# A 64-row matmul into a spare PSUM bank after the second unit of each MLP part

## The chip, the cores and the metric

The kernel runs on one core of one Trainium2 chip. The metric is device time in microseconds (us), the median of several executions; less is better. One further execution was taken with the hardware profiler, and every row below is from that one.

## The reference

Two layers of a decoder trunk over 256 tokens of width 2048, in fp32. Each layer normalises, projects, mixes (attention and RWKV-7 in layer 0, RG-LRU and HGRN2 in layer 1), projects back, and then runs an MLP with a squared ReLU. The change touches the two MLPs alone:

```python
D_MODEL, SEQ, D_FF = 2048, 256, 4 * 2048

def _sq_relu_mlp(h, w1, w2):
    z = jax.nn.relu(h @ w1)
    return (z * z) @ w2

for layer in range(2):
    ...                                   # mixers: x = x + y
    x = x + _sq_relu_mlp(_rms_norm(x, norm_mlp[layer]), w_ff1[layer], w_ff2[layer])
```

## The kernel before

Activations lie transposed: 16 blocks of 128 features, each with 256 tokens. To keep fp32 accuracy, weights and activations are split into a high part and a low part (fp32r). A moving block is `[128, 256 high | 256 low]`.

A **unit** (`unit`, L155) makes one block of 128 output features. It runs 16 **pairs** of matmuls (`mm3`, L147), one pair for each block of the contraction: L152 multiplies the high weights with all 512 moving columns ("the high matmul"), and L153 the low weights with the 256 high columns ("the low matmul"). Each of them loads its own 128x128 weights first. The 32 matmuls of a unit accumulate in one bank of the PSUM pool `pmm`, which has two buffers. Afterwards `evac` (L163) adds the two halves through ScalarE and VectorE.

The weights of a unit come in two halves of 512 KB by SyncE's DMA queue (`load`), and ScalarE (L130) and VectorE (L132) split them. These loads and splits have a high priority, so they run ahead of the matmuls that use them.

`mlp` (L928) has eight **parts** of 16 units each: `up(0) up(1) down(0) up(2) down(1) up(3) down(2) down(3)`. An `up` makes a quarter of the hidden layer, a `down` adds a quarter's contribution to the trunk `xs`. One MLP is 128 units, or 2048 pairs, and both MLPs together are 256 units. Each engine runs its own instructions in order; a tile scheduler sets that order from priorities and from the order of the code.

Other PSUM banks come from `bank` (L112), the pool `pg` with the tags `ga` and `gb`, two buffers each. The mixers use them heavily; in the MLPs nobody does, apart from one matmul of `rstd_of` (L206) while the first unit runs. `ident` is a 128x128 fp32 identity in the tile `con`.

Matmuls whose operands are plain fp32 (not fp32r) appear in the mixers. The ones that matter below: L425 contracts over 64 rows of the array with 128 columns of weights, L520 has 64 moving columns with the whole array, L522 uses 128 rows and 64 columns, L600 128 rows and 32 columns, L477 32 rows and 32 columns, and L206 and L838 use the whole array. In a row of the trace, `64*128` ahead of the shapes says rows and columns of the array.

Of the kernel before, what the change touches and what calls it, by code (L numbers as in the profile page):

```python
# [58 lines left out]
def kernel(  # L59
# [58 lines left out]
    def operand(pool, name):  # L118
        """16 blocks [128, 256 high | 256 low] of a moving operand."""
        return [t[:, k] for t in (half_of(pool, f"{name}_{h}") for h in range(2)) for k in range(8)]  # L120

# [1 line left out]
    def load(src, h, name, pool=None):  # L123
# [11 lines left out]
    def stream(src, name, pool=None):  # L135
        """A chunk of 16 blocks [K 128, 128 columns], in parts of 8 blocks: (high, low) each."""
        out = []
        for h in range(2):
            with tc.high_priority():
                out.append(split(load(src, h, name, pool if h else None), h, name))  # L140
        return out

    def behind():
        """Work of the mixers that yields to the projections that are ready."""
        return tc.high_priority(-120)
# [25 lines left out]
    def sigmoid(dst, src, bias=0.0):  # L171
        """exp(-ln(1 + exp(-x))) of x = src + bias, with x held above -80 where exp(-x) would overflow"""
        V.tensor_scalar(dst, src, bias, -80.0, op0=ALU.add, op1=ALU.max)
        A.activation(dst, dst, AF.Exp, scale=-1.0)
        A.activation(dst, dst, AF.Ln, bias=one_b[: dst.shape[0]])
        A.activation(dst, dst, AF.Exp, scale=-1.0)
# [7 lines left out]

# [1 line left out]
    def rsqrt_of(dst, src, scale, bias, name, pool):  # L186
        """exp(-ln(scale * src + bias) / 2)"""
        l = pool.tile([src.shape[0], src.shape[1]], F32, tag="rsl", name=f"l_{name}", bufs=2 if pool.name == "pn" else 1)
        A.activation(l, src, AF.Ln, bias=bias[: src.shape[0]], scale=scale)
        A.activation(dst, l, AF.Exp, scale=-0.5)  # L190
# [39 lines left out]

# [1 line left out]
    def layer0_mix():  # L232
# [77 lines left out]
    def rwkv_a(pa, gate, hx, scaled, rwp_d, pm_d, nb, first, load_cw):  # L310
# [26 lines left out]
        for j in range(8):  # L337
# [18 lines left out]
            sigmoid(aa, ps2[:, :T], bias=p_("a0", j))  # L356
            # features
            cs = tl("cs", bufs=2, name=f"cs_{j}")
# [19 lines left out]
            with behind():  # L378
# [32 lines left out]
                A.copy(rwp[:, 1796:2052], psg[:, :T])  # L411
                # token major copies
                ptv = bk_(f"ptv_{j}")
# [5 lines left out]
                A.copy(rwp[:, 512:1024], ptb)  # L419
                # products within the chunks  # L420
                for q in range(2):
# [14 lines left out]
    def rw_solve(pb, nb, z_d):  # L436
        """(1 - N)^-1 of the strictly upper triangular N [32, 32] of every partition, in place."""
        for s in range(1, 31):
            n = 31 - s
            tmp = pb.tile([P, 2, T], F32, tag="y", name=f"ztmp_{s}")  # L440
            tv = tmp.rearrange("p r t -> p (r t)")[:, : s * n].rearrange("p (r t) -> p r t", t=n)
            V.tensor_mul(
                tv, nb[:, 0:s, s : s + 1].to_broadcast([P, s, n]),
                nb[:, s : s + 1, s + 1 : 32].to_broadcast([P, s, n]))
            V.tensor_add(nb[:, 0:s, s + 1 : 32], nb[:, 0:s, s + 1 : 32], tv)
        G.memset(nb.rearrange("p r t -> p (r t)")[:, 0 : 1024 : 33], 1.0)
        G.dma_start(z_d, nb)

    def rwkv_b(pb, j, rwp_d, pm_d, z_d, yr):
        """The chunks of two pairs of heads in turn, from the products within the chunks."""  # L450

# [36 lines left out]
        s = None  # L488
# [205 lines left out]

# [1 line left out]
    def layer1_mix(hx, rstd, ym):  # L696
        scaled = scaled_by(rstd)
        with ExitStack() as st:
            hp = st.enter_context(tc.tile_pool(name="hp", bufs=1))
            hgmk = hp.tile([P, 7, P], F32, name="hgmk")  # L700
            nc.scalar.dma_start(hgmk, hgmask)
            lw = hp.tile([P, 2, 8, P], F32, name="lw")
            nc.scalar.dma_start(lw, lru_w)
            prm = hp.tile([P, 8, 8], F32, name="prm")
            # lower bounds of the forget gates: softmax over the two layers
            mxl, e0, e1 = prm[:, 0], prm[:, 1], prm[:, 2]
            V.tensor_max(mxl, p_("lb0"), p_("lb1"))
            V.tensor_sub(e0, p_("lb0"), mxl)
            V.tensor_sub(e1, p_("lb1"), mxl)
            A.activation(prm[:, 1:3], prm[:, 1:3], AF.Exp)  # L710
            V.tensor_add(mxl, e0, e1)
            V.reciprocal(mxl, mxl)
            V.tensor_mul(e0, e0, mxl)
            V.tensor_mul(e1, e1, mxl)
            V.tensor_add(e1, e0, e1)
            lower, oml = prm[:, 1], prm[:, 2]
            V.tensor_sub(lower, e1, e0)
            V.tensor_scalar(oml, lower, -1.0, 1.0, op0=ALU.mult, op1=ALU.add)
            # softplus(-lambda) = max(-lambda, 0) + log1p(exp(-|lambda|)),
            # log1p(e) = 2 atanh(e / (2 + e)) as its series in s = e / (2 + e) <= 1/3  # L720
            sp = prm[:, 3]
            ab = prm[:, 4]
            V.tensor_scalar(ab, p_("lam"), -1.0, None, op0=ALU.mult)
            V.tensor_tensor(sp, ab, p_("lam"), ALU.min)
            A.activation(sp, sp, AF.Exp)
            s2, pl = prm[:, 5], prm[:, 0]
            V.tensor_scalar_add(s2, sp, 2.0)
            V.reciprocal(s2, s2)
            V.tensor_mul(sp, sp, s2)
            V.tensor_mul(s2, sp, sp)  # L730
            V.tensor_scalar(pl, s2, 1.0 / 19, None, op0=ALU.mult)
            for n in range(17, 1, -2):
                V.scalar_tensor_tensor(pl, pl, 1.0 / n, s2, ALU.add, ALU.mult)
            V.scalar_tensor_tensor(sp, pl, 1.0, sp, ALU.add, ALU.mult)
            V.tensor_scalar_max(ab, ab, 0.0)
            V.scalar_tensor_tensor(sp, sp, 2.0, ab, ALU.mult, ALU.add)
            V.tensor_scalar(prm[:, 4], sp, -8.0, None, op0=ALU.mult)
            V.tensor_scalar(prm[:, 5], sp, 8.0, None, op0=ALU.mult)

            at = [hp.tile([P, 384], F32, name=f"at{i}") for i in range(2)]  # L740
            for a in at:
                G.memset(a, 0.0)
            for h in range(8):
                hgrn_head(hp, h, hx, scaled, ym, hgmk, prm, at)
            for q in range(2):
                lru_group(hp, q, hx, scaled, ym, lw, prm)

    def hgrn_head(hp, h, hx, scaled, ym, hgmk, prm, at):
# [29 lines left out]
        with behind():  # L778
# [6 lines left out]
            a = at[h % 2]  # L785
            # pairs within blocks of 64
            for b in range(4):
# [23 lines left out]
                for x, m in enumerate(todo):  # L811
# [3 lines left out]
                    V.copy_predicated(dst, hgmk.bitcast(U32)[:, lvl, None, :].to_broadcast([P, 2, P]), src)  # L815
            # blocks of 64 and of 128 against each other
            eu = tl("he", bufs=2, name=f"heu_{h}")
# [37 lines left out]
    def lru_group(hp, grp, hx, scaled, ym, lw, prm):  # L855
# [5 lines left out]
        for j in js:  # L861
# [15 lines left out]
            scaled(unit(w_in1[33 + 2 * j], hx, f"i1_{33 + 2 * j}"), gate[j], f"lgt{j}")  # L877
        # the activations by table set, in this order
        pin = tc.keep_in_program_order
# [9 lines left out]
        act_set(LN_EXP)  # L889
        # 1 - exp(2 log a) = 2 t / (1 + t), t = tanh(-log a)  # L890
        d = {}
# [16 lines left out]

# [1 line left out]
    def out_proj(xs, w_out, ym, order, acc, hx, gain, name):  # L910
# [17 lines left out]
    def mlp(layer, xs, hx, rstd, nxt, zp, zraw):  # L928
        z = {}

        def up(q):
            zq = z[q] = operand(big if q % 2 == 0 else zp, f"z_{layer}_{q}")
            for k in range(KT):
                n = f"f1_{layer}_{q}_{k}"
                s = evac(unit(w_ff1[layer, q * KT + k], hx, n, pool=zraw), n)
                V.tensor_mul(s, s, rstd)  # L936
                V.scalar_tensor_tensor(s, s, 0.0, s, ALU.max, ALU.mult)
                split_to(zq[k], s)

        def down(q):  # L940
            for c in range(KT):
                n = f"f2_{layer}_{q}_{c}"
                s = evac(unit(w_ff2[layer, q, c], z[q], n, pool=zraw), n)
                V.tensor_add(xs[:, c], xs[:, c], s)
                if q == 3:
# [10 lines left out]

# [1 line left out]
    ym = layer0_mix()  # L958
# [26 lines left out]

# [1 line left out]
def _chunks(w):  # L987
    """[K, N] -> [N / 128, 128, K / 128 * 128]: for each 128 columns the blocks of K, side by side."""
    k, n = w.shape
# [11 lines left out]
def _layout(i):  # L1001
# [53 lines left out]

    # constants of the shapes alone
    con = np.zeros((P, NCON), f32)
# [69 lines left out]
```

## Time and profile before

| what | value |
|---|---|
| median of the timed runs | 2411.09 us (3 runs, 2410.25 to 2414.4) |
| span of the profiled execution | 2435.2 us |
| TensorE (PE) busy in it | 2409.9 us, 99% |
| VectorE, ScalarE busy | 1697.5 us, 1244.4 us |
| first MLP, its matmuls | from about 580 us to about 1304 us |
| second MLP, its matmuls | from about 1720 us to the end |

The profiled execution has a span, from its first instruction to its last; no other time of it is given. A row's start counts from the beginning of the span. PE stands for TensorE's matmuls, and the weight loads have rows of their own. Matmuls overlap in the array, so a matmul's duration is longer than the distance from its start to the next one's. That distance is what a stream of matmuls costs.

### The profile page before, as it was taken

Reading aid. Unit: us, or ns where it says so; the run is one execution under the profiler, and the core shown is the slowest. Engines: PE = TensorE matmul, PEld = TensorE weight load, DVE = VectorE, ACT = ScalarE, POOL = GpSimd, SP = SyncE. Lnnn points to the kernel's source line nnn. Section 1 sums busy time; section 2 is a strip of 40 time slices with the busy share of each in tenths; the row PEclk is TensorE's granted clock in tenths of the full one; section 3 lists DMA queues with packets and bytes.
Section 4 is the critical chain, followed back from the end, with each engine's and each line's share of the span. In section 5 each row is a group of like instructions: output and inputs, shape, how many; then the busy total and the mean of one; then the engine's idle time right before and its main releaser. Section 6 shows DMA issues by size and latency. Waiting matters only on the chain.

```text
span 2435.2 us, 37943 instructions
## 1 busy us (share of the span) xinstructions
PE 2409.9 (99%) x14385; PEld 2087.2 (86%) x14385; DVE 1697.5 (70%) x3006; ACT 1244.4 (51%) x2152; POOL 44.2 (2%) x115
## 2 busy tenths in 40 slices
PE   7999999999999999999999999999999999999999
PEld 6888877789888888888888888889988888888888
DVE  7887745677676566566567888788777667667555
ACT  7554335655444444444456666586544444444443
POOL 0111010000000000000000000000000000000000
PEclk9999989999999999999999999999999999999999
DMA  7666643365555555555555444456556655655564
GB/s 261 211 215 217 221 141 114 115 216 182 185 188 185 187 187 185 189 184 187 185 188 174 156 156 149 152 167 216 183 190 190 191 190 190 190 190 190 190 196 134
DMA packets 125861, 446.75 MB, mean 183 GB/s; under 512 B 14192, under 2 KB 19952, under 8 KB 124016
## 3 DMA queue, kind: packets, MB, share of 16 engines
q1 hardware_dynamic: 115824, 414.04, 53.0%
q0 software_dynamic: 5456, 26.79, 3.0%
q10 hardware_dynamic: 4400, 3.50, 0.4%
q8 instruction: 114, 1.87, 0.3%
q14 instruction: 67, 0.55, 0.1%
HBM read 429.04 MB, written 15.22 MB: 182 GB/s over the span
## 4 chain that ended last, share of the span: by engine, by line
PE 93%; DVE 3%; DMA 2%; ACT 1%; issue 1%; POOL 0%; DVEq 0%; POOLq 0%; SPq 0%; ACTq 0%
PE mm_f L152 39%; PE mm_f L153 20%; PE mm_i L152 13%; PE mm_i L153 7%; PE mm_o L153 2%; PE mm_o L152 2%; PE mm_o L149 1%; PE mm_o L150 1%; PE hl L810 1%; DVE wl_i L132 1%; PE pair L425 1%; PE psx L495 0%; DMA rwp_d<-rwp 0%; PE psu L502 0%; PE psx L493 0%
## 5 line engine op out<-in xcount | busy, mean ns | idle before, releaser
L132 DVE TENSOR_TENSOR wl_f<-raw_f,wh_f 128x1024 fp32r<-128x1024 f32 x512 | 627.2, 1225 | 486.1 <-ACT wh_f L130 486.1
L130 ACT CAST wh_f<-raw_f 128x1024 fp32r<-128x1024 f32 x512 | 538.6, 1052 | 772.9 <-PE mm_f L152 566.4
L152 PE MATMUL mm_f<-hx_m,wh_f 128*128 128x512 f32 x2048 | 717.2, 395 | 0.0
L152 PE MATMUL mm_f<-z,wh_f 128*128 128x512 f32 x2048 | 717.1, 395 | 0.0
L152 PE MATMUL mm_i<-hx_a,wh_i 128*128 128x512 f32 x1536 | 571.3, 409 | 13.1 <-ACT wh_i L130 13.1
L153 PE MATMUL mm_f<-hx_m,wl_f 128*128 128x256 f32 x2048 | 574.7, 281 | 0.0
L153 PE MATMUL mm_f<-z,wl_f 128*128 128x256 f32 x2048 | 574.3, 280 | 0.0
L152 PEld LDWEIGHTS mm_f<-hx_m,wh_f 128*128 128x128 f32 x2048 | 383.9, 187 | 90.0
L152 PEld LDWEIGHTS mm_f<-z,wh_f 128*128 128x128 f32 x2048 | 383.9, 187 | 90.0
L153 PE MATMUL mm_i<-hx_a,wl_i 128*128 128x256 f32 x1536 | 451.6, 294 | 1.3 <-DVE wl_i L132 1.2
L153 PEld LDWEIGHTS mm_f<-hx_m,wl_f 128*128 128x128 f32 x2048 | 387.0, 189 | 0.1
L153 PEld LDWEIGHTS mm_f<-z,wl_f 128*128 128x128 f32 x2048 | 387.0, 189 | 0.0
L152 PEld LDWEIGHTS mm_i<-hx_a,wh_i 128*128 128x128 f32 x1536 | 292.8, 191 | 76.0 <-ACT wh_i L130 14.0
L153 PEld LDWEIGHTS mm_i<-hx_a,wl_i 128*128 128x128 f32 x1536 | 294.3, 192 | 11.0 <-DVE wl_i L132 4.4
L132 DVE TENSOR_TENSOR wl_i<-raw_i,wh_i 128x1024 fp32r<-128x1024 f32 x192 | 234.6, 1222 | 92.2 <-ACT wh_i L130 85.9
L130 ACT CAST wh_i<-raw_i 128x1024 fp32r<-128x1024 f32 x192 | 201.3, 1049 | 183.4 <-PE mm_i L152 169.2
L168 DVE TENSOR_TENSOR s_f<-mm_f,t_f 128x256 f32<-128x256 f32 x256 | 106.7, 417 | 3.0 <-ACT t_f L167 3.0
L132 DVE TENSOR_TENSOR wl_o<-raw_o,wh_o 128x1024 fp32r<-128x1024 f32 x64 | 78.2, 1223 | 29.3 <-ACT wh_o L130 29.0
L130 ACT CAST wh_o<-raw_o 128x1024 fp32r<-128x1024 f32 x64 | 67.1, 1049 | 60.7 <-issue 31.1
L167 ACT COPY t_f<-mm_f 128x256 f32<-128x256 f32 x256 | 93.2, 364 | 4.3 <-PE mm_f L153 4.3
L153 PE MATMUL mm_o<-ym,wl_o 128*128 128x256 f32 x256 | 72.7, 284 | 0.9 <-DVE wl_o L132 0.9
L936 DVE TENSOR_TENSOR s_f<-s_f,rstd_m 128x256 f32<-128x256 f32 x128 | 54.4, 425 | 4.4
(418 smaller groups left out, 2274.7 us busy)
## 6 DMA issues: line engine op xcount, KB each, us to landing
raw_f<-in_w_ff_dram SPq DMA_DIRECT2D x512, 512.0 KB, 4.3
raw_i<-in_w_in_dram SPq DMA_DIRECT2D x192, 512.0 KB, 3.9
raw_o<-in_w_out_dram SPq DMA_DIRECT2D x64, 512.0 KB, 3.9
rwp_d<-rwp POOLq DMA_DIRECT2D x8, 1026.0 KB, 7.1
rwp<-rwp_d POOLq DMA_DIRECT2D x4, 1540.0 KB, 10.6
cw<-in_cmp_w_dram SPq DMA_DIRECT2D x2, 2048.0 KB, 9.2
pm_d<-pm POOLq DMA_DIRECT2D x8, 512.0 KB, 6.3
pm<-pm_d POOLq DMA_DIRECT2D x4, 1024.0 KB, 6.4
```

The lines of the kernel that those rows point to most:

```text
L130: A.copy(wh, raw)
L132: V.tensor_sub(wl, raw, wh)
L149: M.matmul(ps[:, :T], wh, mv[:, :T], start=first, stop=False)
L150: M.matmul(ps[:, :T], wh, mv[:, T:], start=False, stop=False)
L152: M.matmul(ps, wh, mv, start=first, stop=False)
L153: M.matmul(ps[:, :T], wl, mv[:, :T], start=False, stop=last)
L167: A.copy(t, ps[:, T:])
L168: V.tensor_add(s, ps[:, :T], t)
L425: M.matmul(pp[:, c * P : (c + 1) * P], bk[hs, c], ar[hs, c], start=True, stop=True)
L810: M.matmul(pl[:, x * T + i * P : x * T + (i + 1) * P], qk[:, ii], qk[:, ii], start=True, stop=True)
L936: V.tensor_mul(s, s, rstd)
```

## The change

After the second unit of every part (index 1), one matmul takes 64 rows of the identity as weights and 64 rows by 64 columns of it as the moving operand. It writes 128x64 numbers into a buffer of `ga`, and nothing reads them. `keep_in_program_order` ties the new matmuls to their place among themselves. There are 8 in each MLP, 16 in all. The other lines of the diff only drop comments.

```diff
     def mlp(layer, xs, hx, rstd, nxt, zp, zraw):
         z = {}
 
+        def narrow(n):
+
+            ps = bank(f"nar_{n}")
+            tc.keep_in_program_order(M.matmul(ps[:, 0:64], ident[0:64], ident[0:64, 0:64], start=True, stop=True))
+
         def up(q):
...
                 s = evac(unit(w_ff1[layer, q * KT + k], hx, n, pool=zraw), n)
+                if k == 1:
+                    narrow(n)
                 V.tensor_mul(s, s, rstd)
...
                 s = evac(unit(w_ff2[layer, q, c], z[q], n, pool=zraw), n)
+                if c == 1:
+                    narrow(n)
                 V.tensor_add(xs[:, c], xs[:, c], s)
```

In TensorE's order the first part of the second MLP read as follows before, where the second unit (`mm_f_1_0_1`) ends and the third (`mm_f_1_0_2`) begins:

```order
L152 MATMUL mm_f_1_0_1_17778<-hx_m_1_16665,wh_f_1_0_1_1_17787 128x512
L153 MATMUL mm_f_1_0_1_17778<-hx_m_1_16665,wl_f_1_0_1_1_17789 128x256
L152 MATMUL mm_f_1_0_2_17831<-hx_m_0_16664,wh_f_1_0_2_0_17834 128x512
L153 MATMUL mm_f_1_0_2_17831<-hx_m_0_16664,wl_f_1_0_2_0_17836 128x256
L152 MATMUL mm_f_1_0_2_17831<-hx_m_0_16664,wh_f_1_0_2_0_17834 128x512
```

With the change the same place on TensorE reads:

```order
L152 MATMUL mm_f_1_0_1_17794<-hx_m_1_16681,wh_f_1_0_1_1_17803 128x512
L153 MATMUL mm_f_1_0_1_17794<-hx_m_1_16681,wl_f_1_0_1_1_17805 128x256
L934 MATMUL nar_f_1_0_1_17843<-con 128x64
L152 MATMUL mm_f_1_0_2_17849<-hx_m_0_16680,wh_f_1_0_2_0_17852 128x512
L153 MATMUL mm_f_1_0_2_17849<-hx_m_0_16680,wl_f_1_0_2_0_17854 128x256
```

The new matmul (L934) stands exactly between the last low matmul of the second unit and the first high matmul of the third, and it names no wait. It is the same at all 16 places. Apart from these 16 rows, no engine's order differs, and the DMA queues' does not either.

## Rows read from the trace of the kernel before

**Rows 1.** The page: the span, the busy engines, and the granted clock in 40 slices
```profile
span 2435.2 us, 37943 instructions
...
PE 2409.9 (99%) x14385; PEld 2087.2 (86%) x14385; DVE 1697.5 (70%) x3006; ACT 1244.4 (51%) x2152; POOL 44.2 (2%) x115
...
PEclk9999989999999999999999999999999999999999
```

**Rows 2.** TensorE in two stretches, one inside each MLP: busy (matmuls), clock, DMA
```profile
600.00:1290.00 690.00, 690.00 (x3907) 1.00 0.58 186
1730.00:2420.00 690.00, 690.00 (x3983) 1.00 0.60 189
```

**Rows 3.** Groups by line, 600 to 1290 us: busy, mean ns, idle before
```profile
L152 PE MATMUL mm_f<-z,wh_f 128*128 128x512 f32 x984 | 347.8, 399 | 0.0
```

**Rows 4.** The same group, 1730 to 2425 us
```profile
L152 PE MATMUL mm_f<-z,wh_f 128*128 128x512 f32 x1009 | 349.9, 391 | 0.0
```

**Rows 5.** Groups by line, whole span: L206, which runs twice at `ms_m`
```profile
L206 PE MATMUL ms_m<-acc_m,con 128*128 128x256 f32 x4 | 1.4, 431 | 0.0
```

**Rows 6.** Timeline of TensorE around four 64-row matmuls: start, us, what
```profile
175.43 0.28 PE L153 MATMUL mm_i<-hx_a,wl_i 128*128 128x256 f32 x1
175.64 1.16 PE L425 MATMUL pair<-rwp,bk 64*128 64x128 f32 x8
176.72 0.50 PE L152 MATMUL mm_i<-hx_a,wh_i 128*128 128x512 f32 x1
177.06 0.28 PE L153 MATMUL mm_i<-hx_a,wl_i 128*128 128x256 f32 x1
```

**Rows 7.** Timeline around one fp32 matmul of 64 moving columns
```profile
343.43 0.43 PE L520 MATMUL psy<-rwp,st 128*128 128x64 f32 x2
343.79 0.34 PE L522 MATMUL psy<-pm,rwp 128*64 128x64 f32 x4
```

**Rows 8.** Timeline around one whole-array fp32 matmul of 128 columns, L838
```profile
1360.03 0.28 PE L153 MATMUL mm_i<-hx_a,wl_i 128*128 128x256 f32 x1
1360.15 0.38 PE L838 MATMUL hh<-hqs,hks 128*128 128x128 f32 x2
...
1360.60 0.28 PE L153 MATMUL mm_i<-hx_a,wl_i 128*128 128x256 f32 x1
```

**Rows 9.** Timeline around one whole-array fp32 matmul of 256 columns, L206
```profile
1310.56 0.28 PE L153 MATMUL mm_i<-hx_a,wl_i 128*128 128x256 f32 x1
...
1311.34 0.28 PE L153 MATMUL mm_i<-hx_a,wl_i 128*128 128x256 f32 x1
```

**Rows 10.** Groups by line, 178 to 187 us, right behind rows 6
```profile
L152 PE MATMUL mm_i<-hx_a,wh_i 128*128 128x512 f32 x24 | 8.5, 399 | 0.0
```

**Rows 11.** Groups by line, 254 to 264 us, behind L600, which ends at 252.6
```profile
L152 PE MATMUL mm_i<-hx_a,wh_i 128*128 128x512 f32 x24 | 8.5, 398 | 0.0
```

**Rows 12.** Timeline behind 32 matmuls of L477
```profile
392.89 0.39 PE L152 MATMUL mm_i<-hx_a,wh_i 128*128 128x512 f32 x1
...
393.23 0.40 PE L152 MATMUL mm_i<-hx_a,wh_i 128*128 128x512 f32 x1
```

**Rows 13.** Timeline around another four 64-row matmuls of L425
```profile
128.70 0.39 PE L152 MATMUL mm_i<-hx_a,wh_i 128*128 128x512 f32 x1
129.02 1.16 PE L425 MATMUL pair<-rwp,bk 64*128 64x128 f32 x8
130.11 0.39 PE L153 MATMUL mm_i<-hx_a,wl_i 128*128 128x256 f32 x1
```

**Rows 14.** Groups by line, 132 to 142 us, behind rows 13
```profile
L152 PE MATMUL mm_i<-hx_a,wh_i 128*128 128x512 f32 x30 | 10.4, 391 | 0.0
```

**Rows 15.** Groups by line, 1712 to 1722 us, ahead of L206
```profile
L152 PE MATMUL mm_f<-hx_m,wh_f 128*128 128x512 f32 x8 | 2.9, 399 | 0.0
```

**Rows 16.** Timeline: L206 in the first unit of the second MLP
```profile
1722.72 0.70 PE L206 MATMUL ms_m<-acc_m,con 128*128 128x256 f32 x2
```

**Rows 17.** Groups by line, 1724 to 1734 us, behind that L206
```profile
L152 PE MATMUL mm_f<-hx_m,wh_f 128*128 128x512 f32 x30 | 10.4, 391 | 0.0
```

## The prediction

> **What bounds the kernel now.** I read the page first. TensorE is busy 99% of the span, VectorE 70%, ScalarE 51% [rows 1]. So the question in the MLPs is how closely matmul follows matmul. Next I asked for one stretch inside each MLP. In both the engine is never idle and the granted clock is 1.00, the higher of its two levels, 2.4 GHz [rows 2]. No wait appears ahead of the MLPs' matmuls, the idle time before them is 0.0 [rows 3, 4]. Whatever TensorE gets on top in these stages, the time pays in full.
>
> The same two rows show something less expected. In 690 us the first MLP issues 3907 matmuls and the second 3983 [rows 2], with the same instructions, shapes and clock. Per pair that is 690 / (3907 / 2) = 353.2 ns against 690 / (3983 / 2) = 346.5 ns, a difference of 6.7 ns. The modelled duration of the high matmul tells the two cadences apart at a glance: 399 ns in the first MLP, 391 ns in the second [rows 3, 4]. I call them slow and fast. Each lasts through a whole MLP, and since nothing waits there, nothing can end it. The cadence a stream falls into seems to be decided where the stream is broken. At the head of the second MLP the high matmuls still show 399 [rows 15], then comes a single fp32 matmul, L206 [rows 16], and from there on it is 391 [rows 17]. The change breaks the stream 16 times, so it has two prices: that of the break, and that of the cadence afterwards.
>
> **The price of one break.** One plain fp32 matmul of the program is two records: L206 runs once in each layer at this tile, and the group counts four [rows 5]. So each `narrow` adds two weight loads and two matmuls of 64 columns. No row shows a lone matmul of this shape, but all its pieces are there. I measure from the start of the last low matmul of the second unit to the start of the first low matmul of the third. Without a break this is one pair, 0.347 us.
>
> - Into the 64-row shape. Ahead of L425, which uses 64 rows and 128 columns of the array as `narrow` does, 0.21 us pass from the low matmul's start to the first L425 [rows 6]. Between matmuls of the usual shape it is 0.12 us (1360.03 to 1360.15) [rows 8].
> - The two matmuls and the way back. L520 has the same 64 moving columns and is followed by a change of shape. From its first record to the first of L522 0.36 us pass [rows 7].
> - The restart. The first high matmul after L425 starts at 176.72 and its low matmul at 177.06, 0.34 us later [rows 6]. This is one weight load more than in the stream, because nothing could be loaded ahead.
>
> The sum is 0.21 + 0.36 + 0.34 - 0.347 = 0.56 us for each, and 16 of them are **9.0 us**. Nothing hides it, TensorE has no idle time there. Behind the break only the weight stream stands, on engines with 30% to 49% to spare.
>
> The lower bound is a matmul that changes no shape: L838 stretches the distance from low to low to 0.57 us [rows 8], which is 0.22 more than a pair, or 3.6 us for 16. For the upper bound I take L206, four times as many columns, at 0.78 - 0.35 = 0.43 us [rows 9]. To that I add what the two shape changes cost above: 0.21 - 0.12 = 0.09 in front, and 0.1 for emptying plus 0.1 for a bare weight load behind. That gives 0.72, or 11.5 us. I take 9.0, because L425 has the very shape of `narrow` and shows the front and the restart directly.
>
> Why the front and the restart cost so much is what a page states: the Trainium skill, in "TensorEngine Tiling (Array Packing)", Key Properties, says that going over to another tiling mode empties TensorE first. The 0.21 us against 0.12 above agrees, but the page has no price. Without that rule the sum would be the 3.6 us of L838, with it the 9.0 us of the rows.
>
> **The cadence after the break.** What comes behind `narrow` is always a high matmul, L152. The trace has three places where L425 is followed by L152 and a long stream, at 175.6, 202.8 and 229.1 us, and all three go on slow: 399 ns [rows 10] stands for the three. After 32 matmuls of L600, another narrow shape, again followed by L152, it is 398 [rows 11]. The exception is a short stretch of five pairs after L477, where the high matmuls stand 0.34 us apart [rows 12]: fast. Where L425 is followed by the low matmul instead [rows 13], the stream goes on fast, 391 [rows 14], at all five such places. So I expect that an emptied array that restarts with L152 goes on slow.
>
> The first MLP is slow already and gains or loses nothing by that. The second is fast now, and its two units ahead of the first `narrow` stay so. The remaining 126 units are 2016 pairs, and 2016 x 6.7 ns = **13.5 us**.
>
> **The sum.** 9.0 + 13.5 = 22.5 us. The profiled execution would go from a span of 2435.2 to about 2457.7 us. That execution is known by its span alone, which lies 24.1 us above the median of the timed runs, so I carry the difference over: 2411.1 + 22.5 = **2433.6 us**. What a measurement of this kernel can tell from no change is about 0.2%, 4.8 us.
>
> **The rivals.**
>
> - *The break decides for fast.* L206 at the head of the second MLP turned slow into fast [rows 15 to 17], and the five places of L425 with a low matmul behind went fast too. Against it stand the three places with the very order of the change. If all 16 breaks led to fast, the first MLP would win 13.5 us, the second would lose nothing, and with 9.0 us for the breaks the time would be 2411.1 - 4.5 = 2406.6 us. This is the case on the faster side. A part is worth about 256 x 6.7 ns = 1.7 us. Eight parts are slow now, so with n slow parts the change is 9.0 + (n - 8) x 1.7, and it is a gain only when two or fewer of 16 stay slow. I give it 0.18.
> - *The cadence doesn't matter.* The timed runs may not have two cadences (they are 24.1 us shorter than the span), or the breaks may leave about as many parts slow as before. Then the breaks alone remain: 2411.1 + 9.0 = 2420.1 us. The three timed runs lie within 4.2 us, so no MLP went from one cadence to the other among them, which speaks for neither side. I give it 0.25. By a page's rule it would come out this way: the Trainium skill, "TensorE: Matmul & The Clock Gate", Back-to-back issue gap, gives for a warm array a distance that depends on the columns alone. The trace differs, 353.2 against 346.5 ns with the same columns and clock.
> - *The timed runs were fast in both MLPs, and the change makes both slow.* Then 9.0 + 2 x 13.5 = 36.0 us are lost, 2447 us. The shorter timed runs would fit, but nothing else shows it: 0.07.
> - *The break is cheap.* If the shape change costs nothing between matmuls that wait for nobody, 3.6 us and an untouched cadence give 2414.7 us, which is no measurable change. [rows 6] speak against it, although L425 there may have waited for its inputs. I give it 0.05. That the change does nothing at all is excluded, the 16 matmuls stand in TensorE's order.
>
> **How the numbers follow.** The forecast, slow in nearly all parts, has 0.45. Faster by over 0.2% is the fast rival, 0.18; within 0.2% is the cheap break, 0.05; the other three make 0.77 for slower. The likeliest case has its own range of 2425 to 2436: the upper end from 11.5 us for the breaks, the lower one from the cheap bound, 2428, and two parts that stay fast. The range over the cases goes from 2406, which takes in the fast rival, to 2436. It leaves out the case of 2447 and the edges.
>
> **What the changed profile would show.** Right: sixteen pairs of L934 records, each with 0.9 us from low matmul to low matmul instead of 0.35, and 399 ns for the high matmul in the groups of both MLPs, so about 3900 matmuls in 690 us of each. Wrong in the first term: a distance of about 0.57 us around L934. Wrong in the second: 391 behind L934, above all in the first MLP, or a mixture of the two from part to part. The surest way to be wrong is that the cadence depends on more than the instruction that restarts the stream, since I have only a handful of restarts with L152 to go by.

## The result and the profile after

The changed kernel takes 2449.49 us (median of 4 runs, 2445.75 to 2451.64) against 2412.74 us of the kernel before in the same comparison (4 runs, 2410.25 to 2425.98). The ratio is 1.0131, 95% interval 1.0102 to 1.016. That is slower by 36.8 us in the medians, where 22.5 were forecast, and it lies above the range.

The span after, and TensorE's busy time, from the page:

```profile
span 2443.6 us, 38007 instructions
...
PE 2422.0 (99%) x14417; PEld 2085.3 (85%) x14417; DVE 1697.2 (69%) x3006; ACT 1244.0 (51%) x2152; POOL 44.2 (2%) x115
```

The execution with this span took 2445.75 us, so a time is its span and 2.15 us. The profiled span rose by only 8.4 us, from 2435.2 [rows 1]; the timed medians rose by 36.8. The two stretches inside the MLPs (busy, matmuls in brackets, clock, DMA share, GB/s), which answer to [rows 2]:

```profile
600.00:1290.00 690.00, 690.00 (x3900) 1.00 0.57 183
1730.00:2420.00 690.00, 690.00 (x3900) 1.00 0.59 186
```

Both MLPs are slow now, with 3900 matmuls in 690 us, 14 of them records of L934. The first had 3907 already, the second had 3983. The timeline of TensorE around the first new matmul of the second MLP (start, us, line, tile, shapes):

```profile
1721.78 0.28 PE L153 MATMUL mm_f<-hx_m,wl_f 128*128 128x256 f32 x1
1721.99 0.43 PE L934 MATMUL nar_f<-con 64*128 64x64 f32 x2
1722.35 0.50 PE L152 MATMUL mm_f<-hx_m,wh_f 128*128 128x512 f32 x1
1722.68 0.28 PE L153 MATMUL mm_f<-hx_m,wl_f 128*128 128x256 f32 x1
```

From low matmul to low matmul 0.90 us pass, 0.55 more than a pair. The three pieces are the forecast's: 0.21 in front, 0.36 for L934 and the way back, 0.33 for the restart. Ahead of this break the high matmul shows 391 ns and behind it 399 (groups by line, 1713.7 to 1721.9 us, then 1730 to 2420 us):

```profile
L152 PE MATMUL mm_f<-hx_m,wh_f 128*128 128x512 f32 x23 | 8.0, 391 | 0.0
```

```profile
L152 PE MATMUL mm_f<-z,wh_f 128*128 128x512 f32 x1010 | 357.6, 399 | 0.0
```

So both terms of the sum came true in the trace. What did not was the execution that they were added to. The profiled execution of the kernel before had lost time twice. Its first MLP was slow, and ahead of it the granted clock had fallen. TensorE from 300 to 360 us, first of before, then of after:

```profile
300.00:330.00 30.00, 27.16 (x191) 0.77 0.42 130
330.00:360.00 30.00, 28.73 (x232) 0.94 0.52 175
```

```profile
300.00:330.00 30.00, 28.09 (x257) 1.00 0.31 98
330.00:360.00 30.00, 28.74 (x239) 1.00 0.54 181
```

The first MLP's matmuls (instructions by tile: minimum, median and maximum ns, first and last start) begin at 580.0 us before and at 566.3 after:

```profile
L152 PE MATMUL mm_f<-hx_m,wh_f x2048: 391/395/403, 580.0 to 2252.4; 128*128 128x512 f32 x187
```

```profile
L152 PE MATMUL mm_f<-hx_m,wh_f x2048: 390/398/501, 566.3 to 2256.3; 128*128 128x512 f32 x187
```

Of these 13.7 us some 8 arose between 305 and 356 us, where the clock had fallen, and 3.4 around 190 us, where it had fallen too (0.96 from 160 to 200 us); the rest was there within the first 20 us. They hide part of the loss when two single spans are compared. The second MLP, from its L206 (1722.72 [rows 16], 1713.26 after) to the end of the span, went from 712.5 to 730.3 us, 17.8 more: 13.4 for the cadence and 8 x 0.55 = 4.4 for the breaks. The first MLP, slow in both, pays 4.4. 17.8 + 4.4 - 13.7 = 8.5, and the spans differ by 8.4.

### The profile page after: what moved, and what is told of

Its sections match the earlier page's. It is cut to its first block, busy times and chain, and to the rows that moved or that the text cites. A ratio compares the mean times of both kernels' runs of the same rounds, so it can differ in the third digit from the quotient of the medians.

```text
span 2443.6 us, 38007 instructions
## 1 busy us (share of the span) xinstructions
PE 2422.0 (99%) x14417; PEld 2085.3 (85%) x14417; DVE 1697.2 (69%) x3006; ACT 1244.0 (51%) x2152; POOL 44.2 (2%) x115
## 4 chain that ended last, share of the span: by engine, by line
PE 93%; DVE 3%; ACT 1%; DMA 1%; issue 1%; POOL 0%; SPq 0%; ACTq 0%; DVEq 0%; POOLq 0%
PE mm_f L152 39%; PE mm_f L153 20%; PE mm_i L152 13%; PE mm_i L153 7%; PE mm_o L153 2%; PE mm_o L152 2%; PE mm_o L149 1%; PE mm_o L150 1%; PE hl L810 1%; DVE wl_i L132 1%; PE pair L425 1%; PE psx L495 0%; PE psu L502 0%; DVE wl_o L132 0%; DMA rwp_d<-rwp 0%
## 5 line engine op out<-in xcount | busy, mean ns | idle before, releaser
L152 PE MATMUL mm_f<-z,wh_f 128*128 128x512 f32 x2048 | 725.1, 399 | 0.0
L152 PE MATMUL mm_f<-hx_m,wh_f 128*128 128x512 f32 x2048 | 725.0, 399 | 0.0
L152 PE MATMUL mm_i<-hx_a,wh_i 128*128 128x512 f32 x1536 | 565.0, 405 | 10.5 <-ACT wh_i L130 10.5
L152 PEld LDWEIGHTS mm_f<-z,wh_f 128*128 128x128 f32 x2048 | 384.8, 188 | 96.2
L152 PEld LDWEIGHTS mm_f<-hx_m,wh_f 128*128 128x128 f32 x2048 | 384.8, 188 | 96.0
L152 PEld LDWEIGHTS mm_i<-hx_a,wh_i 128*128 128x128 f32 x1536 | 289.6, 189 | 71.7 <-ACT wh_i L130 10.8
L944 DVE SCALAR_TENSOR_TENSOR s_f<-s_f 128x256 f32<-128x256 f32 x128 | 54.4, 425 | 4.4
```

The source lines that it names most:

```text
L152: M.matmul(ps, wh, mv, start=first, stop=False)
```

## The experiments

All were compared with the kernel before on the same chip. For `narrow` I say "break".

### The kernel before, again

The edit is none. 

> The kernel before, once more. Theory (the cadence of each MLP is drawn anew in every execution of the kernel before, and timed runs have it too): times fall on steps 13.5 us apart, about 2410 with both MLPs fast, 2424 with one slow, 2437 with both slow; the profiled execution shows 391 or 399 ns for the high matmul of each MLP and its time agrees with that count. Rival (the profiler alone makes the slow cadence): the timed runs stay at 2410 to 2414, and the profiled one is slow in one MLP again and 24 us longer.

Measured: 10 runs, median 2425.73 (2411.6 to 2429.34), ratio 1.0022 (0.9994 to 1.005). Three of the ten took 2411.6 to 2416.88 us, seven took 2425.23 to 2429.34. Besides these the kernel before ran 21 times more. Sorted by the granted clock of the execution those 21 are:

```
clock 1.0:    2409.91                                                      2423.43
clock 0.999:  2408.37 2408.88 2409.72 2409.91 2411.14 2411.6               2423.57 2423.93 2425.47
clock 0.998:                                                               2427.34
clock 0.997:  2415.23 2415.81 2416.58 2416.75 2417.28                      2427.9 2430.69
clock 0.996:                                                               2431.66
clock 0.995:  2419.67
```

At the three clocks that have executions in both columns, the clusters lie 13.0 to 14.4 us apart in their means, and nothing lies another step higher. The profiled one (span 2425.4, time 2427.53) was slow in the first MLP and fast in the second (groups by line, 600 to 1290 and 1730 to 2410 us):

```profile
L152 PE MATMUL mm_f<-z,wh_f 128*128 128x512 f32 x1011 | 357.4, 399 | 0.0
```

```profile
L152 PE MATMUL mm_f<-z,wh_f 128*128 128x512 f32 x994 | 344.7, 391 | 0.0
```

So the rival falls: seven of the ten runs and eight of the 21 lie in the upper cluster. The theory holds for the first MLP alone. In all twelve profiled executions of this document TensorE's instructions are the same up to the first break. Behind its L206 the first MLP was slow in five of them and fast in seven; the second MLP was fast behind its L206 in all twelve. Here is one of the seven, from "The breaks without a change of shape", between L206 and its first break (575 to 582 us):

```profile
L152 PE MATMUL mm_f<-hx_m,wh_f 128*128 128x512 f32 x21 | 7.3, 391 | 0.0
```

So an execution of the kernel before has none or one of its MLPs slow, and those near 2410 are the ones with both fast. No trace of this kernel shows both fast; it follows from the step, and from "One whole-array break in each MLP" below, whose traced execution is fast in both and lies in the lower cluster.

### One break in each MLP

```diff
-                if k == 1:
+                if k == 1 and q == 0:
                     narrow(n)
...
-                if c == 1:
-                    narrow(n)
```

> One break in each MLP, in its first part, in place of eight. Theory (the break costs 0.56 us once and leaves the whole rest of the MLP slow): 399 ns behind it in both MLPs, 2410 + 27 + 1.1 = 2438 us. Rival (36.7 us over 16 breaks are 2.3 us each, and the cadence is no matter): 2410 + 4.6 = 2415 us.

Measured: 2442.82 us (6 runs, 2439.43 to 2445.04), ratio 1.0095 (1.006 to 1.0129). The executions with a clock of 0.999 took 2439.43 and 2441.13. Behind the break of the second MLP (1730 to 2420 us):

```profile
L152 PE MATMUL mm_f<-z,wh_f 128*128 128x512 f32 x990 | 349.9, 399 | 0.0
```

Two breaks of 16 bring most of the loss. The cadence is the larger part, the breaks themselves the smaller.

### The 16 breaks with a low restart

```diff
 def mm3(...):
             M.matmul(ps, wh, mv, start=first, stop=False)
+        if mid:
+            mid()                    # narrow(n), in the last pair of the second unit
         M.matmul(ps[:, :T], wl, mv[:, :T], start=False, stop=last)
```

> All 16 breaks, each moved ahead by one matmul, between the high and the low matmul of the second unit's last pair, so that the stream restarts with the low one. Theory (the instruction that restarts the stream behind an emptied array decides its cadence): 391 ns behind every break in both MLPs, 2410 + 16 x 0.55 = 2419 us. Rival (every change of the array's shape leaves it slow): 399 ns, 2446 us as with the change.

Measured: 2435.16 us (10 runs, 2430.86 to 2437.8), ratio 1.0062 (1.0038 to 1.0085). Neither the theory's 2419 nor the rival's 2446. The cadence changes over at every one of the 16 breaks. Groups by line of the first part behind a break and of the next (580 to 667 and 670 to 756 us):

```profile
L152 PE MATMUL mm_f<-hx_m,wh_f 128*128 128x512 f32 x247 | 87.3, 399 | 0.0
```

```profile
L152 PE MATMUL mm_f<-hx_m,wh_f 128*128 128x512 f32 x222 | 77.0, 391 | 0.0
```

Half the parts are slow: 2410 + 13.4 + 16 x 0.55 = 2432 us. So the instruction that restarts the stream does not decide by itself, and the cadence from before the break matters, although the array changed its shape twice in between.

### The breaks without a change of shape

```diff
-            tc.keep_in_program_order(M.matmul(ps[:, 0:64], ident[0:64], ident[0:64, 0:64], start=True, stop=True))
+            tc.keep_in_program_order(M.matmul(ps[:, 0:64], ident, ident[:, 0:64], start=True, stop=True))
```

> The breaks where the change has them, but with all 128 rows of the identity, so that the array's shape does not change. Theory (only an emptied array that restarts with the high matmul goes on slow): about 0.22 us for each break, 3.5 us in all, the cadence mixed or as before the break, 2414 to 2430 us. Rival (any break ahead of a high matmul leaves it slow): 399 ns in both MLPs, 2441 us.

Measured: 2443.83 us (4 runs, 2443.3 to 2444.51), ratio 1.01 (1.0057 to 1.0144). The break is cheap, as expected, 1723.23 to 1723.80 or 0.57 us from low to low, 0.22 more than a pair:

```profile
1723.23 0.28 PE L153 MATMUL mm_f<-hx_m,wl_f 128*128 128x256 f32 x1
1723.34 0.33 PE L934 MATMUL nar_f<-con 128*128 128x64 f32 x2
...
1723.80 0.28 PE L153 MATMUL mm_f<-hx_m,wl_f 128*128 128x256 f32 x1
```

These 0.22 us are what the two weight loads of L934 take, from the start of the first to that of the next load:

```profile
1723.23 0.30 PEld L934 LDWEIGHTS nar_f<-con 128*128 128x128 f32 x2
1723.45 0.19 PEld L152 LDWEIGHTS mm_f<-hx_m,wh_f 128*128 128x128 f32 x1
```

But all 16 parts go on slow, and the rival is right: 2410 + 27 + 3.5 = 2440.5 us. The rest is the clock: it was 0.998 in all four executions, and at 0.998 a lower-cluster execution of the kernel before took 2413.07 ("The kernel before, again"). The change of shape costs 0.33 us for each break, which is measured here as 0.55 - 0.22, and the slow cadence comes without it too.

### Setting the fast cadence

One break behind the second unit and one inside the last pair of the third, in the first part of each MLP; the other parts have none.

```diff
-                s = evac(unit(w_ff1[layer, q * KT + k], hx, n, pool=zraw), n)
-                if k == 1:
+                s = evac(unit(..., mid=(lambda: narrow(n)) if k == 2 and q == 0 else None), n)
+                if k == 1 and q == 0:
                     narrow(n)
```

> Two breaks in each MLP, both in the first part: one behind the second unit, as in the change, and one between the high and the low matmul of the third unit's last pair. Theory (a restart with the high matmul always sets slow, a restart with the low one out of slow always sets fast): 391 ns for all the rest of both MLPs in every execution, 2410 + 4 x 0.55 + 0.2 = 2412.5 us with a spread of only the mixers, against a kernel before that steps between about 2410 and 2425. Rival (the toggle of the kernel with low restarts came from the equal distance of its breaks): slow or mixed, up to 2439 us.

Measured: 2418.52 us (12 runs, 2412.28 to 2423.96), ratio 0.9997 (0.9978 to 1.0016). At clocks of 0.999 and 1.0 it took 2412.49 and 2412.28 us; the others had lower clocks. Behind the second break (590 to 1280 us; the second MLP alike):

```profile
L152 PE MATMUL mm_f<-z,wh_f 128*128 128x512 f32 x1018 | 353.0, 391 | 0.0
```

The profiled execution behaved as the theory says. The medians do not tell it from the kernel before, since most of the compared executions of that had both MLPs fast by their times.

### Whole-array breaks with a low restart

The edit is that of the low restart, with `ident, ident[:, 0:64]` as operands. 

> The 16 breaks between a high and a low matmul, with all 128 rows of the identity. Theory (the restart and the cadence before decide, not the array's shape): from break to break the cadence changes over, half the parts slow, each break about 0.22 us. Rival (the change of shape matters for the low restart): one cadence throughout.

Measured: 2418.19 us in one run, clock 0.998. All 16 parts are fast, so the rival is right in that there is one cadence. TensorE from 590 to 1280 and from 1717 to 2400 us:

```profile
590.00:1280.00 690.00, 690.00 (x3988) 1.00 0.60 187
1717.00:2400.00 683.00, 683.00 (x3947) 1.00 0.60 189
```

The first break came out of slow, the 15 others out of fast. The 64-row break with the same restart led out of fast to slow each time ("The 16 breaks with a low restart"), so for this restart the shape of the break matters.

### Two matmuls at each place

```diff
-            tc.keep_in_program_order(M.matmul(ps[:, 0:64], ident[0:64], ident[0:64, 0:64], start=True, stop=True))
+            for i in range(2):
+                tc.keep_in_program_order(M.matmul(ps[:, 64 * i : 64 * i + 64], ident[0:64], ident[0:64, 0:64], start=True, stop=True))
```

> The change with two of its matmuls at each of the 16 places. Theory (0.55 us are two shape changes, a restart and two bare weight loads of 0.11 us each): the second matmul adds two weight loads, 0.22 us, so 0.77 us for each place and all slow behind it; with 16 x 0.22 = 3.5 us on top of the change about 2450 to 2455 us. Rival (each matmul brings its own emptying): 1.1 us for each place, 9 us on top.

Measured: 2441.83 us in one run, less than the change, clock 1.0. The price is the theory's: 1720.97 to 1722.10 is 1.13 us, 0.78 more than a pair.

```profile
1720.97 0.28 PE L153 MATMUL mm_f<-hx_m,wl_f 128*128 128x256 f32 x1
1721.18 0.66 PE L935 MATMUL nar_f<-con 64*128 64x64 f32 x4
...
1722.10 0.28 PE L153 MATMUL mm_f<-hx_m,wl_f 128*128 128x256 f32 x1
```

The cadence is not: in each MLP three parts of eight are fast, among them the second. There (674 to 760 us) the modelled duration is 394 ns with a low matmul of 277, a third pattern with the pace of the fast one:

```profile
L152 PE MATMUL mm_f<-hx_m,wh_f 128*128 128x512 f32 x222 | 77.0, 394 | 0.0
L153 PE MATMUL mm_f<-hx_m,wl_f 128*128 128x256 f32 x222 | 61.5, 277 | 0.0
```

So a high restart does not always lead to slow either. Nor is it the pair of the unit that decides: the break falls in the last pair everywhere, and out of slow it leads to fast six times and to slow four times. What differs is where it meets the slow cadence's own pattern, which repeats every three pairs. The last two high matmuls ahead of the break at 852.99 us, behind which slow goes on, stand 0.35 us apart; those ahead of the break at 944.23, behind which fast follows, 0.37. All ten agree with this.

```profile
852.19 0.40 PE L152 MATMUL mm_f<-hx_m,wh_f 128*128 128x512 f32 x1
...
852.54 0.40 PE L152 MATMUL mm_f<-hx_m,wh_f 128*128 128x512 f32 x1
```

```profile
943.42 0.40 PE L152 MATMUL mm_f<-z,wh_f 128*128 128x512 f32 x1
...
943.79 0.40 PE L152 MATMUL mm_f<-z,wh_f 128*128 128x512 f32 x1
```

### Three distances

In every part a break behind the second unit, and one inside the third unit's last pair, last but one, or last but two (`at=KT - 1 - q % 3` in `up`, `KT - 1 - (q + 2) % 3` in `down`, otherwise as in "Setting the fast cadence"). 

> In every part one break behind the second unit, as in the change, and one between high and low matmul in the third unit, in its last pair, the last but one or the last but two, in turn over the parts; the slow cadence repeats every three pairs, so the second break meets each of its three phases. Theory (out of slow a low restart always sets fast): 391 ns behind all 16 second breaks. Rival (the phase decides): fast behind one or two of the three distances, slow behind the others, the same in all parts with one distance.

Measured: 2442.42 us in one run, clock 0.997, with 32 breaks. The parts with the break in the last pair, in the last but one, and in the last but two, from 600, 690 and 780 us:

```profile
600.00:670.00 70.00, 70.00 (x406) 1.00 0.59 188
690.00:760.00 70.00, 70.00 (x398) 1.00 0.58 185
780.00:850.00 70.00, 70.00 (x405) 1.00 0.59 190
```

The last pair leads to fast (6 of 6), the last but one to slow (4 of 4), the last but two to fast (6 of 6). The rival is right: the same break, with the same restart, out of the same slow cadence, leads to one or the other by the pair in which it falls, that is by its place in the pattern of three.

### One whole-array break in each MLP

The low restart with `ident, ident[:, 0:64]`, in the second unit of the first part alone (`k == 1 and q == 0`). 

> One break in each MLP, with all 128 rows, between the high and the low matmul of the second unit's last pair, the form that was followed by the fast cadence 16 times of 16. Theory (this form always leads to fast, whatever came before, so the MLPs no longer differ from execution to execution): 391 ns behind it in both MLPs, and at a granted clock of 0.999 to 1.0 about 2410 us in every execution, with no second cluster 13.6 us above as the kernel before has it; against the kernel before a ratio of about 0.997. Rival (the first MLP can still come out slow): some executions at 2424 or more at such a clock.

Measured: 2416.3 us (12 runs, 2410.05 to 2421.23) against 2416.62 (17 runs, 2411.28 to 2435.99), ratio 0.999 (0.9968 to 1.0011). The executions at a clock of 1.0 took 2410.05, 2411.18 and 2411.49 us. None of the twelve lies in the upper cluster, where the kernel before had three of 17 (2429.85, 2430.17, 2435.99). Three of 17 against none of twelve could be chance; together with "Setting the fast cadence" it is eight of 34 against none of 24. The ratio of 0.997 did not come: with three of 17 there is too little to win, and the clock spreads both by some 10 us.

The traced execution (2415.83 us, clock 0.997) is fast behind both breaks, in the third pattern, 394 and not the 391 expected (590 to 1280 us; the second MLP alike):

```profile
L152 PE MATMUL mm_f<-z,wh_f 128*128 128x512 f32 x1016 | 352.4, 394 | 0.0
```

At this clock the lower cluster of the kernel before took 2414.41 to 2418.49 us here.

### Eight lengths

The low restart with `ident, con[:, 0:n]`, n = 32, 64, ... 256 over the parts. 

> The same form of break in all 16 parts, but with 32, 64, 96 up to 256 moving columns, growing from part to part, the same in both MLPs. Theory (how long the break lasts against the stream decides the cadence, not the instruction that restarts it): fast and slow mixed over the lengths, the same lengths alike in both MLPs where the cadence ahead of them is alike. Rival (a whole-array break that restarts with the low matmul always sets fast): 391 ns behind all 16.

Measured: 2420.58 us in one run, clock 0.999. In both MLPs 32 columns lead to slow and all the others to fast. Here are the parts with 32 and 64 columns in the first MLP and in the second:

```profile
585.00:665.00 80.00, 80.00 (x455) 1.00 0.58 188
675.00:755.00 80.00, 80.00 (x463) 1.00 0.58 191
1715.00:1795.00 80.00, 80.00 (x455) 1.00 0.58 187
1805.00:1885.00 80.00, 80.00 (x463) 1.00 0.61 190
```

Each part with 32 columns came out of fast, and so did parts with 96 and more that stayed fast. Same place, same restart, same cadence before, another number of columns: the rival falls. But the theory's wording falls as well, since the break of 32 columns and that of 96, each out of fast in the first MLP, last equally long. From the high matmul ahead to the low one behind it is 0.37 us in both:

```profile
580.43 0.39 PE L152 MATMUL mm_f<-hx_m,wh_f 128*128 128x512 f32 x1
580.66 0.30 PE L938 MATMUL nar_f<-con 128*128 128x32 f32 x2
580.80 0.36 PE L155 MATMUL mm_f<-hx_m,wl_f 128*128 128x256 f32 x1
```

```profile
760.09 0.39 PE L152 MATMUL mm_f<-z,wh_f 128*128 128x512 f32 x1
760.32 0.36 PE L938 MATMUL nar_f<-con 128*128 128x96 f32 x2
760.46 0.36 PE L155 MATMUL mm_f<-z,wl_f 128*128 128x256 f32 x1
```

So it is the number of columns that counts here, and not the time by which the stream is held up.

## Why the prediction was wrong

**The base was wrong, and with it the sum.** The step that failed is "so I carry the difference over": the profiled execution lay 24.1 us above the median, and the forecast took this for something that all timed runs save alike, so that the second MLP alone could lose. A time is the span and 2.15 us, so that execution took about 2437.3 us: 13.5 for its slow first MLP and 13.7 ahead of it, most of them where the clock had fallen, on top of some 2410. The three runs shown (2410.25 to 2414.4) belong by their times to the lower cluster, with both MLPs fast; the fourth, 2425.98, lies in the upper one. The change makes both slow: 2410 + 2 x 13.4 + 16 x 0.55 = 2445.6 us, and the two executions at a clock of 1.0 took 2445.75 and 2448.51. This is the third rival, 2447 us, which had 0.07. The row that should have warned me stood in [rows 1], where the clock has an 8 in one slice.

**The price of a break was right**: 0.56 forecast, 0.55 measured, piece by piece. L520, L425 and the restart behind L425 gave it, and the whole-array experiment and the doubled one confirm its parts, 0.33 us for the change of shape and 0.22 for the two weight loads. The 0.1 us for emptying in its upper bound stood on no row; the sum of 9.0 us did not use it.

**The cadence after the breaks came out as forecast, 16 of 16 slow, but not for the reason given.** "An emptied array that restarts with L152 goes on slow" fell. A break without a change of shape goes on slow as well, two matmuls in place of one lead to fast in three parts of eight, and a low restart leads to either. What the runs show is narrower. The cadence follows from the form of the break (its shape, its columns, one matmul or two, what restarts the stream), from the cadence ahead of it and, out of slow, from its place in the pattern of three pairs. Where all of these were the same, so was the outcome, in all 136 breaks of the ten traced kernels that have any. The change's own form went on slow in all 36 cases, here and in three experiments, so its outcome was steady; but the four restarts of the mixers from which I drew the rule, behind L425 and L600, only happened to agree with it. The five places with a low matmul behind L425 are counted wrong: there are ten, six of them with five pairs or more behind, and all are fast.

**The rivals.** "The break decides for fast" did not occur for this form of break, but it does for another, the whole-array one with a low restart. "The cadence doesn't matter" is refuted by the repeated kernel before and by the single break in each MLP. "The break is cheap" holds only without the change of shape.

**What stays open.** Why a saturated stream has two paces at all, and by what mechanism a break leads to one or the other, was not found. That the first MLP of the kernel before differs from execution to execution fits with its L206, which waits for VectorE and so meets the stream at another moment each time; this is argued, not tested. In the twelve traces that moment, counted from the high matmul ahead, lies within 4 ns: 400 ns in the five slow ones, 399, 401 or 402 in the seven fast ones.

## What to carry to other kernels

A profile is one execution. Before a term is added to the median of other runs, check that this execution is like them: its own time against theirs, its clock slice by slice, and the pace of equal stages against each other. Where two stages of equal work run at different paces without a wait, that difference may change from run to run, and a kernel should be compared by clusters, not by one median. A matmul that uses part of the array costs its two changes of shape besides its weight loads, 0.33 and 0.22 us here, even where nobody reads its result.

## What was unexpected of the hardware

With the clock granted in full, a stream of equal matmuls without a wait ran at 346.5 or at 353.2 ns a pair and kept its pace for more than 2000 pairs. One inserted matmul could change the pace for all that followed, and two changes of the array's shape did not erase what came before: with a low restart and 64 rows, fast followed slow and slow followed fast at all 16 breaks.
